# The down projection of pairs 1 to 8 in seven block products, spread between the products of gate and up, in a float32 encoder on one Trainium2 core

## The chip, the core and the metric

The kernel runs on one core of a Trainium2 chip. Its engines are named as the profile names them: PE (TensorE, matrix products; PEld is its loading of the stationary operand), DVE (VectorE), ACT (ScalarE), POOL (GpSimd) and SP (SyncE, which here only issues DMAs). The metric is the device time of one execution in microseconds (us); lower is better.

## The reference

Two layers of a hybrid encoder act on 768 tokens (512 of a sample, 256 of a prompt) of width 1024. Each layer has two feed-forward blocks with a mixer (attention and a state-space scan) between them. Only the feed-forward block is touched here:

```python
def swiglu_ffn(x, w_gate, w_up, w_down):
    return (jax.nn.silu(x @ w_gate) * (x @ w_up)) @ w_down

for l in range(DEPTH):                      # DEPTH = 2, D_FF = 2816
    x = layer_norm(ALPHA * x + 0.5 * swiglu_ffn(x, ...ffn1...), ln1_g[l], ln1_b[l])
    mix = hybrid_mixer(x, ...)
    x = layer_norm(ALPHA * x + mix, ln2_g[l], ln2_b[l])
    x = layer_norm(ALPHA * x + 0.5 * swiglu_ffn(x, ...ffn2...), ln3_g[l], ln3_b[l])
```

## The kernel before

**Arithmetic.** A float32 operand is held as two parts in the PE's format: a high part (an ACT cast) and a low part (DVE: the value less its high part). One product is three matmuls: high by high, high by low, low by high.

**Tiling.** The hidden width of 2816 is 22 tiles of 128, taken as 11 pairs p = 0 to 10; there are four such feed-forward stages. For a pair, gate and up are each a 2 by 2 block matrix times the input (tokens in two halves of 384, depth in two halves of 512). Pair 0 is plain (`plain_pair`). Pairs 1 to 10 (`fast_pair`) use the Strassen-Winograd form: seven block products instead of eight, 14 for gate and up together, each 4 x 3 = 12 matmuls of 384 columns (L444). The block sums of the input (T1 to T4) are made once per stage by `sums_of_x`, on DVE, ACT and POOL. Those of the weights, S1 to S4, are DVE additions of 128x512 (L89).

**Hidden values.** `block` evicts gate (silu on ACT) and up (a DVE product) into `sg`, a [128, 2, 768] buffer in the arena. `finish` (L366) splits all of `sg` into one of two `hbuf` pairs by one cast of 1536 columns on ACT (L368) and one subtraction on DVE (L369).

**Down.** `down` (L484) is one block of matmuls for a pair: for 6 token tiles, 2 hidden tiles and 3 part products into two banks of 512 columns, that is 72 matmuls of 512 columns (L499), each tile ending in two DVE evictions into `y` (L506). By `down_after` the block of pair 0 stands behind pair 0, the blocks of pairs 1 to 8 one pair late (that of pair p behind the products of pair p + 1), and those of pairs 9 and 10 together at the end.

**Weights.** `WeightStream` keeps the order of use. SP loads 1 MB slabs (two gate and up slabs and one down slab a pair) into two raw buffers. `split` makes the two parts of a unit of 128x512 (ACT L110, DVE L111) in one of nine rotating buffers, up to five units ahead. POOL issues no DMA.

**Order.** The program is written in order of dependence; a scheduler then sets the order of each engine's queue, in which instructions run strictly one after the other. Semaphores join the queues.

Of the kernel before, what the change touches and what calls it, by code (L numbers as in the profile page):

```python
# [50 lines left out]
class WeightStream:  # L51
    """Weights in the order of their use: DMA into raw slabs, then an exact split in two float32r parts.

    A unit is a slice of its slab, or a sum of slices (the block sums of a Strassen-Winograd product).
    """
# [36 lines left out]

    def split(self, upto):
        nc = self.nc
        while self.nsplit <= min(upto, len(self.units) - 1):
            u = self.units[self.nsplit]
            n = u.get("n", UNIT)
            self.dma(u["slab"] + 1)
            raw = self.source(u["slab"], u["what"], n)
            if u.get("place") is not None:  # L100
                hi, lo = self.places[u["place"]]
            else:
                t = self.pool.tile([P, 2 * ZN], F32R, tag="w", name="w", bufs=NWBUF)
                hi, lo = t[:, :n], t[:, n : 2 * n]
            g = u.get("scale")
            if g is not None:
                nc.scalar.activation(hi, raw, AF.Copy, scale=g)
                nc.vector.scalar_tensor_tensor(lo, raw, g, hi.bitcast(F32), op0=ALU.mult, op1=ALU.subtract)
            else:
                nc.scalar.copy(hi, raw)  # L110
                nc.vector.tensor_sub(lo, raw, hi.bitcast(F32))  # L111
            u["hl"] = (hi, lo)
            self.nsplit += 1

# [8 lines left out]
def trunk(ctx, tc, x_in, w_gu, w_dn, w_xbc, w_z, w_qk, w_v, w_out, ln_gb, ln_gbc, conv_wb, gmix, smalls, bias, y_out):  # L123
# [57 lines left out]
    # the order of the block products of gate (0) and up (1)  # L181
    PRODUCTS = ((0, 0), (0, 1), (0, "S2"), (0, "S1"), (0, "S3"), (1, 0), (0, 3), (0, "S4"),
                (1, "S2"), (1, 1), (1, "S3"), (1, "S1"), (1, 3), (1, "S4"))
    DCH = [(p, p + 1) for p in range(NPAIR - 2)] + [(NPAIR - 2, NPAIR)]

    def down_after(p):
        return [0] if p == 0 else [p - 1] if 1 < p < NPAIR - 1 else [len(DCH) - 1] if p == NPAIR - 1 else []

    for l in range(DEPTH):
        for w in range(2):  # L190
            if w == 1:
                slab(w_xbc[l, 0], range(4))
                for j in range(2):
                    slab(w_z[l, j], range(4), n=ZN)
                for j in range(1, 4):
                    slab(w_xbc[l, j], range(4))
                for j in range(4):
                    slab(w_qk[l, j], range(4))
                for j in range(2):
                    slab(w_v[l, j], range(4))  # L200
                for j in range(4):
                    i = slab(w_out[l, j])
                    for u in range(4):
                        k = 2 * j + u // 2
                        n = 4 * j + u - NWBUF
                        units.append(dict(slab=i, what=u, scale=gmx[:, l, k : k + 1], place=n if n >= 0 else None))
            dn = lambda a, b: [slab(w_dn[l, w, p], range(4)) for p in range(a, b)]
            for p in range(NPAIR):
                if p < NPLAIN:
                    a, b = slab(w_gu[l, w, p, 0]), slab(w_gu[l, w, p, 1])  # L210
                    units.extend(dict(slab=q, what=2 * m + k) for m in range(2) for q in (a, b) for k in range(2))
                else:
                    ab = slab(w_gu[l, w, p, 0]), slab(w_gu[l, w, p, 1])
                    units.extend(dict(slab=ab[m], what=x) for m, x in PRODUCTS)
                for c in down_after(p):
                    for i in range(*DCH[c]):
                        slab(w_dn[l, w, i], range(4))
    ws = WeightStream(nc, wpool, slabs, units, [at(o_sum + i * UNIT, UNIT) for i in range(3)])
# [5 lines left out]
    # ---- input  # L224
# [24 lines left out]
    def split_x(ps, k0, nk, c0, n):  # L249
        """PSUM columns -> the two parts of X"""  # L250
# [11 lines left out]
    def to_x(src, t, tags=("A", "A")):  # L262
        """token-major [128, 1024] -> X[:, :, tile t]"""
# [860 lines left out]
```

## Time and profile before

| | us |
|---|---|
| median of 3 runs | 2917.91 |
| lowest and highest run | 2914.05, 2918.11 |
| span of the profiled execution | 2913.6 |
| PE busy | 2869.5 (98%) |
| DVE busy | 1993.7 (68%) |
| ACT busy | 1300.1 (45%) |
| POOL busy | 135.5 (5%) |

Of the profiled execution the page gives the span alone; the runs lie 0.5 to 4.5 us above it, 4.3 at the median. Busy time counts from the start of an instruction to its end, and successive instructions of an engine overlap a little, so what an engine can take is read from the starts of instructions that follow one another without a wait. Start and end of matmuls are modelled; the distance of two starts is what one costs.

### The profile page before, as it was taken

Reading aid. Unit: us, or ns where it says so; the run is one execution under the profiler, and the core shown is the slowest. Engines: PE = TensorE matmul, PEld = TensorE weight load, DVE = VectorE, ACT = ScalarE, POOL = GpSimd, SP = SyncE. Lnnn points to the kernel's source line nnn. Section 1 sums busy time; section 2 is a strip of 40 time slices with the busy share of each in tenths; the row PEclk is TensorE's granted clock in tenths of the full one; section 3 lists DMA queues with packets and bytes.
Section 4 is the critical chain, followed back from the end, with each engine's and each line's share of the span. In section 5 each row is a group of like instructions: output and inputs, shape, how many; then the busy total and the mean of one; then the engine's idle time right before and its main releaser. Section 6 shows DMA issues by size and latency. Waiting matters only on the chain.

```text
span 2913.6 us, 39357 instructions
## 1 busy us (share of the span) xinstructions
PE 2869.5 (98%) x15382; PEld 2568.4 (88%) x15382; DVE 1993.7 (68%) x3659; ACT 1300.1 (45%) x2587; POOL 135.5 (5%) x193
## 2 busy tenths in 40 slices
PE   8999999999999999999989999999999999999998
PEld 7999999888767899999879999998887678999997
DVE  7767666868545966666697666667685459666666
ACT  4443333657456443333544333335583554433333
POOL 3000000100000100000030000000000011000000
PEclk9999999999999999999999999999999999999999
DMA  3221212224323121212212212222243231212212
GB/s 118 73 81 65 73 63 97 99 90 140 130 85 122 61 75 64 79 60 72 73 49 74 81 59 72 73 88 102 94 138 134 82 134 59 73 58 73 73 58 87
DMA packets 59451, 246.19 MB, mean 84 GB/s; under 512 B 7104, under 2 KB 19584, under 8 KB 37760
## 3 DMA queue, kind: packets, MB, share of 16 engines
q1 hardware_dynamic: 59264, 243.67, 24.4%
q8 instruction: 120, 1.97, 0.3%
q14 instruction: 67, 0.55, 0.1%
HBM read 224.67 MB, written 18.97 MB: 84 GB/s over the span
## 4 chain that ended last, share of the span: by engine, by line
PE 91%; DVE 5%; ACT 2%; issue 1%; POOL 1%; DMA 0%; SPq 0%; DVEq 0%; POOLq 0%; ACTq 0%
PE psA L444 40%; PE psB L499 12%; PE psC L499 12%; PE psA L346 6%; PE psA L848 5%; PE psA L1003 5%; PE psA L655 2%; PE psB L938 2%; PE psA L876 2%; PE psC L967 2%; PE psB L956 1%; DVE w L111 1%; PE psC L791 1%; PE psA L259 1%; PE psC L743 0%
## 5 line engine op out<-in xcount | busy, mean ns | idle before, releaser
L444 PE MATMUL psA<-XH,w 128*128 128x384 f32 x2560 | 701.4, 338 | 0.0
L110 ACT CAST w<-wraw 128x512 fp32r<-128x512 f32 (+1 forms) x544 | 333.1, 622 | 563.4 <-PE psB L499 381.3
L111 DVE TENSOR_TENSOR w<-wraw,w 128x512 fp32r<-128x512 f32 (+1 forms) x544 | 377.2, 703 | 252.2 <-ACT w L110 246.1
L444 PEld LDWEIGHTS psA<-XH,w 128*128 128x128 f32 x2560 | 468.2, 188 | 1.8
L444 PE MATMUL psA<-XL,w 128*128 128x384 f32 x1280 | 432.2, 338 | 0.0
L110 ACT CAST w<-arena 128x512 fp32r<-128x512 f32 x320 | 194.7, 621 | 216.1 <-PE psA L444 177.0
L111 DVE TENSOR_TENSOR w<-arena,w 128x512 fp32r<-128x512 f32 x320 | 216.9, 689 | 79.8 <-ACT w L110 67.4
L346 PE MATMUL psA<-XH,w 128*128 128x256 f32 (+1 forms) x1056 | 244.5, 338 | 4.9 <-DVE XH L311 4.9
L499 PE MATMUL psB<-w,h0h 128*128 128x512 f32 x576 | 229.7, 399 | 14.6 <-ACT h0h L368 14.6
L506 DVE SCALAR_TENSOR_TENSOR arena<-psB,arena 128x512 f32<-128x512 f32 x216 | 148.7, 688 | 139.0 <-PE psB L499 138.3
L444 PEld LDWEIGHTS psA<-XL,w 128*128 128x128 f32 x1280 | 240.7, 188 | 1.7
L499 PE MATMUL psC<-w,h0h 128*128 128x512 f32 x576 | 228.1, 396 | 0.0
L454 ACT COPY arena<-psA 128x384 f32<-128x384 f32 x240 | 115.1, 479 | 241.0 <-PE psA L444 241.0
L346 PEld LDWEIGHTS psA<-XH,w 128*128 128x128 f32 x1056 | 170.9, 192 | 27.3 <-DVE XH L311 6.3
L459 DVE TENSOR_TENSOR arena<-arena,psA 128x384 f32<-128x384 f32 x240 | 132.5, 552 | 84.1 <-ACT arena L454 45.8
L499 PE MATMUL psB<-w,h1h 128*128 128x512 f32 x480 | 189.5, 395 | 0.0
L499 PE MATMUL psC<-w,h1h 128*128 128x512 f32 x480 | 188.1, 392 | 0.0
L444 PE MATMUL psA<-T2h,w 128*128 128x384 f32 x640 | 177.2, 338 | 0.0
L444 PE MATMUL psA<-T4h,w 128*128 128x384 f32 x640 | 176.7, 337 | 0.0
L444 PE MATMUL psA<-T3h,w 128*128 128x384 f32 x640 | 176.4, 336 | 0.0
L346 PE MATMUL psA<-XL,w 128*128 128x256 f32 (+1 forms) x528 | 152.5, 338 | 3.3 <-DVE XL L312 3.3
L506 DVE SCALAR_TENSOR_TENSOR arena<-psC,arena 128x512 f32<-128x512 f32 x216 | 147.2, 681 | 0.0
(308 smaller groups left out, 5425.3 us busy)
## 6 DMA issues: line engine op xcount, KB each, us to landing
wraw<-in_w_gu_dram SPq DMA_DIRECT2D x86, 1024.0 KB, 4.9
wraw<-in_w_dn_dram SPq DMA_DIRECT2D x44, 1024.0 KB, 4.9
e<-ac_d SPq DMA_DIRECT2D x48, 256.0 KB, 3.4
wraw<-in_w_xbc_dram SPq DMA_DIRECT2D x8, 1024.0 KB, 4.9
wraw<-in_w_qk_dram SPq DMA_DIRECT2D x8, 1024.0 KB, 4.9
arena<-in_bias_dram SPq DMA_DIRECT2D x64, 128.0 KB, 2.1
wraw<-in_w_out_dram SPq DMA_DIRECT2D x8, 1024.0 KB, 4.8
arena<-in_ln_gb_dram SPq DMA_DIRECT2D x6, 1024.0 KB, 5.8
```

The lines of the kernel that those rows point to most:

```text
L110: nc.scalar.copy(hi, raw)
L111: nc.vector.tensor_sub(lo, raw, hi.bitcast(F32))
L346: t_.matmul(ps[:, o : o + b - a], w[:, k % 4], xx[:, k, a:b], start=(k == 0 and part == 0 and i == 0), stop=(k == KD - 1 and part == 1))
L444: t_.matmul(ps, wx[:, k], xx[:, k], start=first and k == 0 and i == 0, stop=k == 3 and i == 2, skip_group_check=not first)
L454: s_.copy(t, banks[m, 1])
L459: v_.tensor_add(src, src, ps)
L499: t_.matmul(ps[n], hx, units[2 * i + n][wx], start=(i == 0 and wi == 0), stop=(i == nf - 1 and wi == 2))
L506: v_.scalar_tensor_tensor(sl, ps[n], 0.5, sl, op0=ALU.mult, op1=ALU.add)
L655: t_.matmul(ps[:, : ZN // 2], xx[:, k % 4], wx[:, n * (ZN // 2) : (n + 1) * (ZN // 2)], start=(k == 0 and wi == 0), stop=(k == KD - 1 and ...
L848: t_.matmul(ps[r][:, : b - a], w[:, k % 4], xx[:, k, a:b], start=(k == 0 and part == 0 and i == 0), stop=(k == KD - 1 and part == 1))
L876: t_.matmul(ps, xx[:, k, cols], wx, start=(k == 0 and wi == 0), stop=(k == KD - 1 and wi == 2))
L1003: t_.matmul(p[n], xx[:, k, cols], wo[2 * k + n][wx], start=(i == 0 and wi == 0), stop=(i == KD - 1 and wi == 2))
```

## The change

Three things change together.

**Down in seven products.** For pairs 1 to 8 the hidden block matrix (tokens in two halves, hidden tiles in two) and the down weights (hidden tiles in two, columns in two) also go through the Strassen-Winograd form. `finish` now makes seven hidden parts of 128x384 (`hs`; A11, A12, A22 and four sums that POOL forms in place in `sg`), each with a cast and a subtraction. `split_down` makes seven weight parts with four DVE sums in place in the raw slab. `down_units` yields 21 pieces (three token tiles of 128 by seven products), each three matmuls of 512 columns and one DVE eviction into `y`. They are popped two at a time behind products 2 to 12 of the next pair. Pairs 0, 9 and 10 keep the plain form, with hidden parts of 384 columns.

**Low parts by transfers.** For units with `acc` (S1, S3 and S4 of gate and of up, and the last four of the seven down parts: ten a pair) the DVE subtraction goes. ACT writes minus the high part into the low part, and a DMA issued by POOL adds the raw value to it.

**Buffers.** Nine rotating weight buffers become twelve fixed places: five for gate and up, used in turn with four units ahead, and seven for down. Gate products are all ahead of up products now (before, they were interleaved).

```diff
+    def parts(self, raw, place, n=UNIT, acc=False, scale=None):
...
+        elif acc:
+            nc.scalar.copy(hi, raw)
+            nc.scalar.activation(lo, hi.bitcast(F32), AF.Copy, scale=-1.0)
+            nc.gpsimd.dma_start(lo, raw, accum_op=ALU.add)
...
+    def split_down(self, slab, i):
+        b11, b12, b21, b22 = (self.raw[slab][:, k * UNIT : (k + 1) * UNIT] for k in range(4))
+        sub = self.nc.vector.tensor_sub
+        if i == 2:
+            sub(b11, b12, b11)
+            sub(b12, b22, b12)
+        if i == 3:
+            sub(b11, b22, b11)
+        if i == 6:
+            sub(b21, b21, b11)
+        raw = (b11, b21, b11, b11, b22, b12, b21)[i]
+        return self.parts(raw, NGU + i, acc=i > 2)
...
+    PRODUCTS = [(m, x) for m in range(2) for x in (0, 1, "S2", "S1", "S3", 3, "S4")]
+    DOWN = (("A11", 1, ((0, 0),)), ("A12", 2, ((0, 0),)), ("S1", 3, ((1, 1),)), ("S2", 1, ((0, 1),)),
+            ("S4", 3, ((0, 1),)), ("S3", 1, ((1, 1),)), ("A22", 1, ((1, 0),)))
...
         def finish(p):
-            hh, hl = hbuf[p % 2]
-            s_.copy(hh, sg)
-            v_.tensor_sub(hl, sg, hh.bitcast(F32))
+            if p == 0 or p >= NPAIR - 2:
...
+            a11, a12, a21, a22 = hblock(0, ha), hblock(1, ha), hblock(0, hb), hblock(1, hb)
+            put_h(0, a11)
+            put_h(1, a12)
+            put_h(2, a22)
+            g_.tensor_add(a22, a21, a22)
+            g_.tensor_sub(a21, a11, a21)
+            put_h(3, a22)
+            g_.tensor_sub(a11, a22, a11)
+            put_h(4, a11)
+            g_.tensor_sub(a12, a12, a11)
+            put_h(5, a21)
+            put_h(6, a12)
...
-                product(ws.get(1, 5)[0], x, banks[m, b], first)
+                product(ws.get(1, NGU - 1)[0], x, banks[m, b], first)
...
+                if first_slab is not None:
+                    if i == 9:
+                        ws.dma(first_slab + 1)
+                    if i >= 10:
+                        dnw.setdefault(p, [])
+                        for k in range(2 * (i - 10), min(2 * (i - 9), NDN)):
+                            dnw[p].append(ws.split_down(first_slab, k))
+                if i >= 2:
+                    for _ in range(min(2, len(units_))):
+                        units_.pop(0)()
...
+        def down_units(p):
...
+                        for k, (hx, wx) in enumerate(((hh, wh), (hh, wl), (hl, wh))):
+                            t_.matmul(ps, hx, wx, start=first and k == 0, stop=k == 2, skip_group_check=not first)
+                        for half, n in blocks:
+                            sl = y[:, q + 3 * half, n * 512 : (n + 1) * 512]
+                            v_.scalar_tensor_tensor(sl, ps, 0.5, sl, op0=ALU.mult, op1=ALU.add)
```

Two places in the queues show the move. In all rows `w` is a weight part, `hNh` and `hNl` the high and low part of hidden part N (in the order of `put_h` after the change), `T3` a block sum of the input, `arena` holds `sg`, the weight sums and `y`.

The first place is the seam between two pairs. ACT before, where pair 3 of the first stage ends and pair 4 begins:

```order
L454 COPY arena<-psA 128x384
L110 CAST w<-wraw 128x512
L110 CAST w<-arena 128x512 x3
L368 CAST h1h<-arena 128x1536
L110 CAST w<-wraw 128x512 x2
```

ACT after, at the same seam (the order is the same at the later seams):

```order
L102 CAST w_100<-wraw 128x512
L103 ACTIVATE w_100<-w_100 128x512
L106 CAST w_90<-wraw 128x512
L512 COPY arena<-psA 128x384
L407 CAST h3h<-arena 128x384
L102 CAST w_89<-arena 128x512
L407 CAST h4h<-arena 128x384
L407 CAST h5h<-arena 128x384
L407 CAST h6h<-arena 128x384
L103 ACTIVATE w_89<-w_89 128x512
```

One cast of `sg` has become seven, of which the last four read what POOL forms; the negated copy for the unit in `w_89` (S3 of gate) now stands behind the last of them. POOL after, at the same seam (before, POOL had nothing between the pairs):

```order
L104 DMA w_93<-arena 128x512
L104 DMA w_100<-wraw 128x512
L420 TENSOR_TENSOR arena<-arena 128x384
L421 TENSOR_TENSOR arena<-arena 128x384
L423 TENSOR_TENSOR arena<-arena 128x384
L425 TENSOR_TENSOR arena<-arena 128x384
L104 DMA w_89<-arena 128x512
L104 DMA w_91<-arena 128x512
```

The transfer that completes `w_89` stands behind the four hidden sums; so it does at seven of the eight seams of a stage. PE after, in pair 4, up to the first use of `w_89`:

```order
L502 MATMUL psA<-XL,w_93 128x384
L502 MATMUL psA<-XH,w_93 128x384
L571 MATMUL psC<-w_96,h3h 128x512 x2
L571 MATMUL psC<-w_96,h3l 128x512
L571 MATMUL psB<-w_97,h4h 128x512 x2
L571 MATMUL psB<-w_97,h4l 128x512
L502 MATMUL psA<-T3h,w_89 128x384
L502 MATMUL psA<-T3l,w_89 128x384
```

The down pieces now stand between product 3 (`w_93`) and product 4 (`w_89`, with T3) of the next pair, not behind all fourteen.

The second place is the start of a stage, where pair 0 ends. PE before, from the last plain matmuls on (19 of L444 stand there in all, then the down block with h0):

```order
L346 MATMUL psA_406<-XH_67,w_393 128x512
L346 MATMUL psA_407<-XH_67,w_393 128x256
L444 MATMUL psA_696<-XH_67,w_634 128x384
L444 MATMUL psA_696<-XL_68,w_634 128x384
L444 MATMUL psA_696<-XH_67,w_634 128x384 x2
```

PE after, at the same place:

```order
L383 MATMUL psA_418<-XH_67,w3_92 128x512
L383 MATMUL psA_419<-XH_67,w3_92 128x256
L593 MATMUL psB_602<-w5_94,h0h_177 128x512
L593 MATMUL psC_603<-w6_95,h0h_177 128x512
L593 MATMUL psB_602<-w5_94,h0l_178 128x512
L593 MATMUL psC_603<-w6_95,h0l_178 128x512
L593 MATMUL psB_618<-w5_94,h0h_177 128x512
L593 MATMUL psC_619<-w6_95,h0h_177 128x512
L593 MATMUL psB_602<-w7_96,h1h_179 128x512
```

The first product of pair 1 is gone from ahead of the down block; eight matmuls with the first hidden tile stand there, and then the second hidden tile is needed.

## Rows read from the trace of the kernel before

**Rows 1.** The page, part 1: busy us (share of the span) xinstructions.

```profile
PE 2869.5 (98%) x15382; PEld 2568.4 (88%) x15382; DVE 1993.7 (68%) x3659; ACT 1300.1 (45%) x2587; POOL 135.5 (5%) x193
```

**Rows 2.** Busy time by stretch: stretch, its us, PE, PEld, DVE, ACT, POOL, clock, DMA.

```profile
276.00:322.00 46.00, 46.00 (x242) 42.95 (x241) 31.29 (x50) 16.67 (x29) 0.00 (x0) 1.00 0.20 69
```

**Rows 3.** Timeline, ACT, the cast of the hidden values (start, us, instruction, [idle before]).

```profile
318.41 1.48 ACT L368 CAST h0h<-arena 128x1536 fp32r<-128x1536 f32 x1 [1.63 <-DVE arena L463]
...
364.43 1.48 ACT L368 CAST h1h<-arena 128x1536 fp32r<-128x1536 f32 x1 [1.63 <-DVE arena L463]
```

**Rows 4.** Timeline, PE, starts of two products and of two token tiles of down.

```profile
290.73 0.34 PE L444 MATMUL psA<-T2h,w 128*128 128x384 f32 x1
...
292.84 0.34 PE L444 MATMUL psA<-XH,w 128*128 128x384 f32 x1
...
315.96 0.39 PE L499 MATMUL psB<-w,h1h 128*128 128x512 f32 x1
...
318.73 0.40 PE L499 MATMUL psB<-w,h1h 128*128 128x512 f32 x1
```

**Rows 5.** Timeline, DVE, instructions that follow one another, 384 and 512 columns.

```profile
290.93 0.55 DVE L459 TENSOR_TENSOR arena<-arena,psA 128x384 f32<-128x384 f32 x1 [0.27 <-PE psA L444]
...
317.83 0.55 DVE L463 TENSOR_TENSOR arena<-arena 128x384 f32<-128x384 f32 x1
318.30 0.68 DVE L89 TENSOR_TENSOR arena<-arena,wraw 128x512 f32<-128x512 f32 x1
318.90 0.68 DVE L506 SCALAR_TENSOR_TENSOR arena<-psB,arena 128x512 f32<-128x512 f32 x1
```

**Rows 6.** Timeline, ACT, 384 and 512 columns (the x2 row: two casts).

```profile
305.71 0.48 ACT L454 COPY arena<-psA 128x384 f32<-128x384 f32 x1 [0.93 <-PE psA L444]
306.08 0.62 ACT L110 CAST w<-wraw 128x512 fp32r<-128x512 f32 x1
...
331.12 1.15 ACT L110 CAST w<-wraw 128x512 fp32r<-128x512 f32 x2 [11.23 <-PE psB L499]
```

**Rows 7.** Timeline, POOL, sums of 384 columns in `sums_of_x`, first stage.

```profile
35.70 7.43 POOL L427 TENSOR_TENSOR arena<-XL 128x384 f32<-128x384 f32 x1 [4.84 <-DVE T3l L416]
43.09 1.02 POOL L424 TENSOR_TENSOR arena<-XH,XL 128x384 f32<-128x384 f32 x1
...
46.66 1.33 POOL L424 TENSOR_TENSOR arena<-XH,XL 128x384 f32<-128x384 f32 x1
```

**Rows 8.** Timeline, DVE, beside those of rows 7.

```profile
40.37 1.88 DVE L111 TENSOR_TENSOR w<-wraw,w 128x512 fp32r<-128x512 f32 x3
43.30 1.22 DVE L416 TENSOR_TENSOR XL<-arena,XH 128x384 fp32r<-128x384 f32 x1 [1.05 <-ACT XH L415]
...
47.03 1.37 DVE L428 TENSOR_TENSOR arena<-arena 128x384 f32<-128x384 f32 x1
```

**Rows 9.** DMA issues: line, count, KB each, median us from issue to landing.

```profile
e<-ac_d SPq DMA_DIRECT2D x48, 256.0 KB, 3.4
...
sz_d<-arena SPq DMA_DIRECT2D x12, 256.0 KB, 2.0
arena<-sz_d SPq DMA_DIRECT2D x12, 256.0 KB, 2.7
```

**Rows 10.** Timeline, PE, the first matmul of down behind pair 0, four stages.

```profile
57.00 0.80 PE L499 MATMUL psB<-w,h0h 128*128 128x512 f32 x1 [3.62 <-ACT h0h L368]
57.59 0.63 PE L499 MATMUL psC<-w,h0h 128*128 128x512 f32 x1
...
980.40 0.50 PE L499 MATMUL psB<-w,h0h 128*128 128x512 f32 x1 [1.57 <-ACT h0h L368]
...
1507.54 0.80 PE L499 MATMUL psB<-w,h0h 128*128 128x512 f32 x1 [7.81 <-ACT h0h L368]
...
2431.55 0.50 PE L499 MATMUL psB<-w,h0h 128*128 128x512 f32 x1 [1.63 <-ACT h0h L368]
```

**Rows 11.** Busy time by stretch behind the first two of rows 10 (columns as rows 2).

```profile
57.00:60.00 3.00, 3.00 (x7) 2.44 (x8) 3.00 (x5) 1.15 (x3) 0.00 (x0) 0.50 0.00 0
60.00:63.00 3.00, 3.00 (x9) 2.41 (x9) 0.99 (x2) 1.65 (x3) 0.00 (x0) 0.52 0.00 0
980.00:990.00 10.00, 9.60 (x42) 7.86 (x43) 9.65 (x16) 3.96 (x9) 0.00 (x0) 1.00 0.00 0
```

More of the change, by code (lines that the diff above doesn't have):

```diff
@@ L97, in split @@
             n = u.get("n", UNIT)
-            self.dma(u["slab"] + 1)
+            self.dma(u["slab"] + u.get("next", 1))
             raw = self.source(u["slab"], u["what"], n)
[L100 to L112, printed above, removed]
-            self.nsplit += 1
+            u["hl"] = self.parts(raw, u["place"], n, u.get("acc", False), u.get("scale"))
+            self.nsplit += 1
+    def split_down(self, slab, i):
[10 more added lines that the diff above has]
+        return self.parts(raw, NGU + i, acc=i > 2)
     def get(self, n=1, ahead=0):
@@ L203, in trunk @@
                     for u in range(4):
[L204 to L207, printed above, removed]
+                        k, n = 2 * j + u // 2, 4 * j + u
+                        units.append(dict(slab=i, what=u, scale=gmx[:, l, k : k + 1], place=n - 8 if n >= 8 else n + 8))
@@ L208, in trunk @@
+                ring[0] = NGU - 1
             for p in range(NPAIR):
-                if p < NPLAIN:
-                    a, b = slab(w_gu[l, w, p, 0]), slab(w_gu[l, w, p, 1])
-                    units.extend(dict(slab=q, what=2 * m + k) for m in range(2) for q in (a, b) for k in range(2))
-                else:
[L213 to L217, printed above, removed]
@@ L218, in trunk @@
-    ws = WeightStream(nc, wpool, slabs, units, [at(o_sum + i * UNIT, UNIT) for i in range(3)])
+                a, b = slab(w_gu[l, w, p, 0]), slab(w_gu[l, w, p, 1])
+                if p == 0:
+                    units.extend(dict(slab=q, what=2 * m + k, place=cyc(NGU)) for m in range(2) for q in (a, b) for k in range(2))
+                    slab(w_dn[l, w, p], range(4))
+                    for k, u in enumerate(units[-4:]):
+                        u["place"] = NGU + k
+                else:
+                    ab = (a, b)
+                    units.extend(dict(slab=ab[m], what=x, acc=x in ("S1", "S3", "S4"), place=cyc(NGU), next=int(i >= NGU - 1))
+                                 for i, (m, x) in enumerate(PRODUCTS))
+                    if p < NPAIR - 2:
+                        dn_slab[l, w, p] = slab(w_dn[l, w, p])
@@ L220, in trunk @@
+            for p in range(NPAIR - 2, NPAIR):
+                slab(w_dn[l, w, p], range(4))
+            for k, u in enumerate(units[-8:]):
+                u["place"] = NGU + k if k < NDN else NGU - 1
+            ring[0] = NGU - 1 if w == 1 else NW - 1
+    wt = [pers.tile([P, 2 * ZN], F32R, name=f"w{i}") for i in range(NW)]
+    ws = WeightStream(nc, wpool, slabs, units, [at(o_sum + i * UNIT, UNIT) for i in range(3)], wt)
     y = at(o_y, NT * DM).rearrange("p (t d) -> p t d", t=NT)
@@ L354, in ffn @@
         hpool = hp.enter_context(tc.tile_pool(name="hpool", bufs=1))
-        hbuf = [tuple(hpool.tile([P, 2, T], F32R, name=f"h{i}{j}") for j in "hl") for i in range(2)]
+        hs = [tuple(hpool.tile([P, HT], F32R, name=f"h{i}{j}") for j in "hl") for i in range(8)]
         tpool = tp.enter_context(tc.tile_pool(name="tpool", bufs=1))
@@ L481, in fast_pair, with run, down @@
                     saved[m, "d"] = True
-            finish(p)
-        def down(c):
-            a, b = DCH[c]
-            last = c == len(DCH) - 1
+                if first_slab is not None:
[8 more added lines that the diff above has]
+                        units_.pop(0)()
+            assert not units_
+            finish(p)
+        dnw = {}
+        def down_units(p):
+            out = []
+            for q in range(3):
+                banks = {}
+                for i, (part, b, blocks) in enumerate(DOWN):
+                    def run(q=q, i=i, part=part, b=b, blocks=blocks, banks=banks):
+                        first = b not in banks
+                        if first:
+                            banks[b] = bank("B" if b == 1 else "C")
+                        ps = banks[b]
+                        hh, hl = (x[:, q * P : (q + 1) * P] for x in hs[HPART[part]])
+                        wh, wl = dnw[p][i]
+                        for k, (hx, wx) in enumerate(((hh, wh), (hh, wl), (hl, wh))):
[3 more added lines that the diff above has]
+                            v_.scalar_tensor_tensor(sl, ps, 0.5, sl, op0=ALU.mult, op1=ALU.add)
+                    out.append(run)
+            return out
+        def down(a, b):
+            last = b == NPAIR
             nf = 2 * (b - a)
```

92 lines of the change are left out of this document (56 added, 36 removed).

## The prediction

> **What bounds the kernel now.** I read the page's busy times first: PE is busy 98% of the span [rows 1]. That is a mean, so I then read one pair in the middle of a stage by the busy time of its stretch: 46.00 of 46.00 us on PE, DVE 31.29, ACT 16.67, POOL nothing, the clock at 1.00, which is the upper of its two levels (2.4 GHz) [rows 2]. In these stretches only fewer matmuls, or shorter ones, save time. The period of a pair is the distance of two casts of the hidden values, 364.43 - 318.41 = 46.02 us [rows 3]. It is made up of 14 products of 292.84 - 290.73 = 2.11 us each (12 matmuls, 0.176 each), 29.5 us, and six token tiles of down of 318.73 - 315.96 = 2.77 us each (12 matmuls, 0.23 each), 16.6 us [rows 4]; the two make 46.1.
>
> **What the change takes away.** Down of a pair goes from 72 matmuls to 3 x 7 x 3 = 63. Nine matmuls of 0.23 us are 2.07 us a pair; 8 pairs in 4 stages are 32, so 66.2 us go from PE. All of it lies on the bounding engine. PE's floor for a pair becomes 29.5 + 63 x 0.23 = 44.0 us.
>
> **What it adds to DVE and ACT.** Instructions of 512 columns follow each other on DVE in 0.60 us, of 384 in 0.47 [rows 5]. Before, a pair has 18 low parts, 8 sums and 12 evictions of 512, ten of 384 and one of 1536: 38 x 0.60 + 10 x 0.47 + 1.7 = 29 us. After, it has 11 low parts, 12 sums and 21 evictions of 512, ten and seven of 384: 44 x 0.60 + 17 x 0.47 = 34.4 us of 44. ACT: 21 casts and 10 negated copies of 512 at 0.53 (a pair of casts takes 1.15, less the overlap) and 17 of 384 at 0.37 to 0.43 [rows 6], about 23 us of 44. Neither becomes the bound by its sum; I cost these at nothing, with PE's 44 us as the cover. Where that cover is thin is the order, at the seam.
>
> **The seam, step by step** (time from the end of a pair's last product, t = 0). Product 4 of the next pair needs the S3 unit, whose place is freed only by that last product. PE gets there after four products and four down pieces: 4 x 2.11 + 12 x 0.23 = 11.2, and the low part is wanted two matmuls later, at t = 11.55. Ahead of that low part stand, each queue in its order:
> - DVE: 0.2 after the product (an addition started 290.93 - 290.73 = 0.2 behind the start of PE's next product [rows 4, 5]), then add, h1l, multiply, h2l. Three distances of 0.47 and one full 0.55 make 2.2. Only then may POOL overwrite the block.
> - POOL: four hidden sums. Such an addition takes 1.02 alone and 1.33 in turn with DVE [rows 7], whose own 0.55 becomes 1.22 to 1.37 at the same time [rows 8]. I take 4 x 1.33, because DVE has low parts to make there, and 0.6 for one DVE instruction ahead of the first: 5.9, so t = 8.1. The bounds are 4 x 1.02 (t = 6.3) and a longer hold, below.
> - ACT: the cast of h6 (0.37) and behind it the negated copy (0.62), 1.0: t = 9.1.
> - The adding transfer, 256 KB, from POOL's queue. No row shows one. The nearest are SP's transfers of 256 KB: 2.0, 2.7 and 3.4 us to landing [rows 9]. Bounds: 2.0, and 3.4 with another 1.0 for POOL (one of its own additions in rows 7), 4.4. A gain is excluded, as PE waits for the landing or doesn't. I take 3.2, near the upper row, because POOL must issue it and it reads its target too: t = 12.3.
>
> The low part is then 0.8 us late. The order has this at seven seams of a stage, 28 in all (at the first, the transfer stands ahead of the four sums): 28 x 0.8 = 22 us come back. The other nine transfers of a pair either stand ahead of the hidden sums or are wanted two products later and more; copy, negated copy and transfer are 0.6 + 0.6 + 3.2 = 4.4 us against four products, at least 8.4, so they cost nothing while POOL issues them in time. Behind the waiting transfer POOL has only that of S4, and ACT has S4's cast and the copy of product 2's bank, which PE needs for product 4 anyway.
>
> A page of the Trainium skill (DMA: Bandwidth & Descriptors, section Anatomy of one DMA — SWDGE (gpsimd) path) prices a transfer from POOL's queue at about 2.0 us plus its bytes over 436 GB/s. Worked out from it (an estimate) this one takes 2.6 us, the low part is 0.15 us late, and the sum below would be 18 us lower. No run here shows such a transfer yet, and an addition may cost more than a copy.
>
> **The start of a stage.** Before, the first product of pair 1 (20 matmuls of 0.176, 3.5 us) covers part of the wait for the hidden cast; still PE idles 3.62, 1.57, 7.81 and 1.63 us [rows 10]. After, 8 matmuls of 0.23 (1.8 us) stand there, then PE needs the second hidden tile. It hangs on the same multiply, with a cast of 384 columns for one of 1536 (1.0 sooner) but with two hidden and two weight low parts more ahead of it on DVE (2.1 later). Loss: 3.5 - 1.8 + 1.1 = 2.8 us, in four stages 11 us. Bounds: 0 if DVE waits there anyway, 23 if the short idle times grow to where the clock falls (below). I take 11, the sum from the order.
>
> **The sum.** Against the profiled span: 2913.6 - 66.2 + 22 + 11 = 2880.4; the median of the runs lies 4.3 above that span, so 2884.7, 33 us or 1.1% below the median.
>
> **Rivals.**
> 1. The transfers are hidden: POOL's sums at 1.02 and a transfer of 2.0 to 2.7 land at t = 9.3 to 10.0. Then 2917.9 - 66.2 + 0 to 11 = 2852 to 2863. For it: POOL shows 1.02. Against it: rows 7 and 8 show POOL and DVE in each other's way wherever both work.
> 2. The wait gives all back: at (66.2 - 11) / 28 = 1.97 us a seam the time is that of before. It needs t = 13.5, so 1.2 more than I take, well inside the bounds. Between 1.75 and 2.2 it is 2912 to 2924.
> 3. Slower, by a longer wait at the same seam: with the transfer at 4.4 and two DVE instructions more in POOL's way (1.2), t is 14.7, 3.1 late: 2917.9 - 66.2 + 88 + 11 = 2951. From 2.2 us late on this decides.
> 4. Much slower, by the clock: behind an idle time of 3.62 us PE ran at 0.50 and 0.52 of its clock (the lower level, 1.2 GHz) for some 6 us, but at 1.00 behind 1.57 [rows 10, 11]. That loses about 2.9 us more. If POOL's sums are held as one was, 7.43 us, while DVE ran low parts without a pause [rows 7, 8], the wait reaches 3.6 and more: 28 x (3.6 + 2.9) = 182, so 2917.9 - 66.2 + 182 + 23 = 3057. Against it: DVE itself waits for these sums at the seam, so it must pause. Of POOL's issuing, a page of the Trainium skill (SBUF — State Buffer, section SBUF: two separate sides) says that DVE instructions in its two-port mode keep POOL from writing a transfer's descriptors, and names a copy within SBUF as such; the pair has none of these on DVE, so by the page the issue itself isn't held, and this rival rests on the sums alone.
> 5. The change doesn't do what it says, or the pieces don't fit between the products: the order shows 63 down matmuls a pair in place, so only 1 in 100.
>
> **How the numbers follow.** A difference of 0.2% (about 6 us) is what a measurement of this kernel can tell from no change. My forecast, a partial gain between 2864 and 2912, has 0.37, and 2885 is its value. Rival 1 has 0.18, rival 2 0.12, rival 3 0.20, rival 4 0.12, rival 5 (no change) 0.01. Faster by over 0.2%: 0.37 + 0.18 = 0.55. Within: 0.12 + 0.01 = 0.13. Slower: 0.20 + 0.12 = 0.32. The range goes from 2856, the middle of rival 1, to 2965, the far side of rival 3; about 0.08 lie below and 0.12, rival 4, above.
>
> **What would show it.** In a pair of the changed kernel: the period by the first hidden cast, 44.0 + 0.8; the waits of PE at T3 with the low part, released by a POOL transfer, and its time from issue to landing; POOL's four sums at the seam, 1.0 or 1.3 each or far longer; DVE near 34 us a pair by starts; PE's clock at 1.00. I am wrong if PE waits elsewhere, on a bank of the down pieces or on DVE, if the transfer lands in under 2.4 us or takes over 4.4, or if the clock falls in the pairs.

## The result and the profile after

| | before | after |
|---|---|---|
| median, us | 2916.8 (4 runs) | 3128.8 (4 runs) |
| span of the profiled execution | 2913.6 | 3131.5 |
| PE busy | 2869.5 | 2905.8 |
| PE idle (span less busy) | 44.1 | 225.7 |
| mean granted clock | 0.995 | 0.962 |

After is slower by 7.3%: the ratio is 1.0731, with a 95% interval of 1.0716 to 1.0747. The forecast was 2885.

The page of after, part 1 (busy us, share, instructions; before: [rows 1]), its DMA issues (count, KB each, median us to landing), and its waits of PE (us in total, times, longest):

```profile
PE 2905.8 (93%) x15094; PEld 2567.7 (82%) x15094; DVE 2223.1 (71%) x4031; ACT 1588.3 (51%) x3279; POOL 597.5 (19%) x689
...
w<-arena POOLq DMA_DIRECT2D x240, 256.0 KB, 4.0
...
w<-wraw POOLq DMA_DIRECT2D x128, 256.0 KB, 4.3
...
PE psA L502 <- DMA w<-arena: 129.1, 30, 5.8
PE psB L593 <- ACT h1h L407: 24.7, 4, 6.6
PE psA L502 <- ACT w L106: 13.9, 4, 3.7
```

Nine matmuls a pair are gone (15382 - 15094 = 288 = 9 x 32), yet PE was busy 36 us longer. One pair, from one cast of h1 to the next, and its seam (columns as [rows 2]):

```profile
206.75:258.67 51.92, 47.15 (x233) 42.81 (x232) 39.37 (x62) 24.79 (x50) 13.83 (x15) 0.93 0.47 112
...
219.00:223.50 4.50, 0.23 (x2) 0.00 (x0) 0.42 (x1) 0.87 (x2) 0.02 (x1) 0.76 1.02 237
223.50:230.00 6.50, 6.44 (x22) 5.80 (x23) 5.05 (x9) 1.52 (x3) 0.00 (x0) 0.64 0.03 6
```

A pair takes 51.9 us, before 46.0 [rows 2, 3]. PE stands still for over 4 us and then runs at 0.64 of its clock, the lower level for most of the stretch. The timeline of that seam, all engines (start, us, instruction, [idle before <- what ended it]):

```profile
209.89 1.34 POOL L420 TENSOR_TENSOR arena<-arena 128x384 f32<-128x384 f32 x1
...
213.73 0.33 SPq L69 DMA_DIRECT2D wraw<-in_w_gu_dram  x1
...
214.03 1.35 POOL L425 TENSOR_TENSOR arena<-arena 128x384 f32<-128x384 f32 x1
...
214.56 0.33 SPq L69 DMA_DIRECT2D wraw<-in_w_dn_dram  x1
...
215.41 0.51 ACT L407 CAST h6h<-arena 128x384 fp32r<-128x384 f32 x1 [0.50 <-POOL arena L425]
...
215.82 0.63 ACT L103 ACTIVATE w<-w 128x512 fp32r<-128x512 f32 x1
...
216.90 0.88 POOL L104 DMA_DIRECT2D w<-arena  x1 [1.52 <-PE psA L502]
...
223.56 1.01 PE L502 MATMUL psA<-T3h,w 128*128 128x384 f32 x2 [4.33 <-DMA w<-arena]
...
224.95 0.69 DVE L90 TENSOR_TENSOR arena<-wraw 128x512 f32<-128x512 f32 x1 [5.53 <-DMA w<-arena]
```

The transfer of gate's S3 part is issued at 216.90 and lands 6.6 us later (the view of L104 gives 6.6 for this one). PE waits 4.33 us for it, DVE 5.53 us, because a sum of up's weights may not overwrite one that a transfer still reads. The wait of PE is there at 28 seams, 3.8 to 5.8 us each; that is 127 of the 129.1 us. The down slab, issued 2.3 us ahead of the transfer, lands at 222.3, the transfer 1.2 us behind it.

**Where 218 us of span went.** Idle time grew by 181.6: some 127 at the seams, 10 at the stage starts (24.7 less the 14.6 of [rows 10]), 14 in the second fast pair of each stage (ACT w L106), the rest in waits of 2.5 us and less. Busy time grew by 36.3, although the work shrank by 67 (the last run below has PE busy 2802.4): so some 103 us were lost at the lower clock. Spread over 28 seams, 4 starts and 4 second pairs, that is 2.9 us each on the mean.

### The profile page after: what moved, and what is told of

It reads as the page before. It is cut to its first block, busy times and chain, and to the rows that moved or that the text cites. A ratio compares the mean times of both kernels' runs of the same rounds, so it can differ in the third digit from the quotient of the medians.

```text
span 3131.5 us, 41384 instructions
## 1 busy us (share of the span) xinstructions
PE 2905.8 (93%) x15094; PEld 2567.7 (82%) x15094; DVE 2223.1 (71%) x4031; ACT 1588.3 (51%) x3279; POOL 597.5 (19%) x689
## 3 DMA queue, kind: packets, MB, share of 16 engines
q1 hardware_dynamic: 59264, 243.67, 23.1%
q0 software_dynamic: 52992, 96.49, 17.7%
## 4 chain that ended last, share of the span: by engine, by line
PE 59%; DVE 14%; DMA 12%; issue 7%; POOL 5%; ACT 3%; POOLq 0%; DVEq 0%; SPq 0%; ACTq 0%
PE psA L502 19%; DMA w<-arena 9%; PE psA L383 5%; PE psB L571 5%; PE psA L1094 5%; PE psC L571 4%; PE psA L940 4%; DVE w L107 3%; PE psB L593 2%; PE psC L593 2%; DVE arena L574 2%; PE psA L747 2%; PE psB L1029 2%; PE psA L967 2%; PE psC L1058 2%
## 5 line engine op out<-in xcount | busy, mean ns | idle before, releaser
L106 ACT CAST w<-wraw 128x512 fp32r<-128x512 f32 (+1 forms) x512 | 308.8, 620 | 332.7 <-PE psA L502 203.5
L104 POOL DMA_DIRECT2D w<-arena x240 | 213.2, 888 | 1110.8 <-ACT w L103 461.2
L502 PE MATMUL psA<-T3h,w 128*128 128x384 f32 x640 | 214.9, 402 | 130.9 <-DMA w<-arena 127.2
L574 DVE SCALAR_TENSOR_TENSOR arena<-psB,arena 128x512 f32<-128x512 f32 x384 | 262.6, 684 | 41.6 <-PE psB L571 40.6
L90 DVE TENSOR_TENSOR arena<-wraw 128x512 f32<-128x512 f32 x160 | 110.2, 689 | 239.6 <-DMA w<-arena 190.6
L102 ACT CAST w<-arena 128x512 fp32r<-128x512 f32 x240 | 148.2, 618 | 239.6 <-PE psA L502 221.5
L502 PEld LDWEIGHTS psA<-T3h,w 128*128 128x128 f32 x640 | 141.1, 230 | 144.8 <-DMA w<-arena 136.5
L103 ACT ACTIVATE w<-w 128x512 fp32r<-128x512 f32 x368 | 225.2, 628 | 3.9
L512 ACT COPY arena<-psA 128x384 f32<-128x384 f32 x240 | 113.2, 472 | 210.0 <-PE psA L502 210.0
L574 DVE SCALAR_TENSOR_TENSOR arena<-psC,arena 128x512 f32<-128x512 f32 x288 | 194.6, 685 | 13.0 <-PE psC L571 6.6
L306 POOL TENSOR_TENSOR stat<-stat,cst 128x1 f32<-128x1 f32 x60 | 26.2, 437 | 885.1 <-ACT arena L908 415.5
L104 POOL DMA_DIRECT2D w<-wraw x128 | 110.6, 921 | 398.7 <-DVE wraw L127 274.1
```

The lines of the kernel that those rows point to most:

```text
L103: nc.scalar.activation(lo, hi.bitcast(F32), AF.Copy, scale=-1.0)
L104: nc.gpsimd.dma_start(lo, raw, accum_op=ALU.add)
L502: t_.matmul(ps, wx[:, k], xx[:, k], start=first and k == 0 and i == 0, stop=k == 3 and i == 2, skip_group_check=not first)
L574: v_.scalar_tensor_tensor(sl, ps, 0.5, sl, op0=ALU.mult, op1=ALU.add)
```

## The experiments

Every time stands beside about 2915 us of before on the same chip.

**One part undone: S3 by VectorE (e1).**

```diff
-acc=x in ("S1", "S3", "S4")
+acc=x in ("S1", "S4") or (x == "S3" and m == 1)
```

> One part undone: the low part of gate's S3 alone is made by a VectorE subtraction again (0.68 us), the other nine still by adding transfers. Theory (seam): 28 seams lose the 4.5 us that PE waits for the landing of this low part and the 2.9 us that each half-clock stretch behind it costs, 28 x 7.4 = 207, so 3129 - 207 = 2922 us, clock back at 0.985 or more. Rival (all transfers are late): the wait moves to gate's S4, whose transfer is issued 1.3 us after, and over half stays: 3020 us or more. Rival (VectorE bound): VectorE, held by the sum temps that transfers still read, is late at the evictions, 1 to 2 us a pair: 2950 to 2980 us.

Measured 3111.1 us. My theory fell. The wait at T3 is gone, and 3.1 us stand a few instructions later. PE's largest wait, and the timeline at the seam:

```profile
PE psC L571 <- DVE arena L574: 108.5, 33, 5.7
...
223.90 0.69 DVE L90 TENSOR_TENSOR arena<-wraw 128x512 f32<-128x512 f32 x1 [2.99 <-DMA w<-arena]
...
225.85 0.50 PE L571 MATMUL psC<-w,h6h 128*128 128x512 f32 x1 [3.13 <-DVE arena L574]
```

DVE's queue runs in order. A sum (L90) waits for a temporary that S4's transfer still reads, the evictions (L574) stand behind it, and PE waits for their bank. The late transfers have two victims, PE and DVE. My second rival had named DVE and these evictions, but at 1 to 2 us a pair; it is 3.1 us here and 108.5 in all, so the time came out far above that rival's.

**Why the transfer lands late (e2, e5, e14, e13).** Rows of after put two slab loads of 1 MB 2.3 and 3.2 us ahead of it. In e2 and e5 the down slab was to be held by a DVE write into its buffer, behind product 5 and 7; the scheduler put both writes at the same early place.

```diff
+if hold:
+    self.nc.vector.memset(t[:, :1], 0.0)
 self.nc.sync.dma_start(t[:, : ap.shape[1]], ap)
...
-next=int(i >= NGU - 1)
+next=int(i >= NGU - 1 and (i < 7 or p >= NPAIR - 2))
...
+if i == 5:
+    ws.dma(first_slab, hold=True)
```

e5 has `i == 7` where e2 has `i == 5`.

> All ten transfers stay; only the load of the next down slab (1 MB), which SyncE issues 2 to 3 us ahead of the late transfer, is held until after product 5 by a VectorE write of one column into the slab's buffer. Theory (DMA engines shared): the transfer's time to landing falls from 6.6 us to about 3.2 to 3.5, PE waits about 1.2 us, the clock doesn't fall: 3129 - 28 x (3.3 + 2.9) = 2955 us. Rival (the transfer is slow by itself, its issue and its own queue): landing stays at 6 us and more, 3120 to 3135 us.

> All as in the changed kernel, but the load of the next down slab is held until after product 7, some 9 us behind the late transfer instead of 2.3 us ahead of it (held until after product 5 it started 0.4 us behind, and the transfer took 7.7 us to land). Theory (the transfer shares the DMA engines with the slab and comes last): landing of gate's S3 part 3.5 to 4.2 us after its issue, PE waits 1 to 1.7 us, no fall of the clock: 3129 - 28 x (3 + 2.9) = 2965 us. Rival (the transfer is slow by itself, or VectorE's wait for the sum temps is the true limit): 3080 us or more.

Measured 3148.5 and 3143.8 us: the load starts 0.4 us behind the transfer, which in e2 then takes 7.7 us. The hold didn't do its work, so this decides nothing. e14 ties the load to the result of the waiting product:

```diff
-next=int(i >= NGU - 1)
+next=int(i >= NGU - 1 and (i < 7 or p >= NPAIR - 2))
...
+if i == 5:
+    ws.dma(first_slab, after=saved[0, "S3"][:, :8])
...
+if after is not None:
+    self.nc.sync.dma_start(t[:, :8], after)
```

> All ten transfers and the order of PE, ACT, VectorE and POOL almost as in the changed kernel; the load of the next down slab is made to follow the product that waits (a 4 KB transfer out of that product's saved result into the slab's buffer goes ahead of it). The two holds before did not move it: the load started 0.4 us behind the late transfer. Theory (the late transfer lands last because it shares the DMA engines with the slab loads issued 2.3 and 3.2 us ahead of it): landing 3.3 to 4 us after the issue instead of 6.6, PE waits 1 to 1.7 us, no fall of the clock, 3129 - 28 x (3 + 2.9) = 2965 us. Rival (transfer slow by itself): landing 6 us or more, 3120 us or more.

Measured 3067.4 us. Timeline of e14 at the seam (its lines stand 2 below those of after):

```profile
212.41 0.88 POOL L106 DMA_DIRECT2D w<-arena  x1 [1.52 <-PE psA L504]
...
215.78 0.62 PE L504 MATMUL psA<-T3h,w 128*128 128x384 f32 x2 [1.05 <-DMA w<-arena]
...
217.35 0.69 DVE L92 TENSOR_TENSOR arena<-wraw 128x512 f32<-128x512 f32 x1 [2.59 <-DMA w<-arena]
...
219.30 0.73 PE L575 MATMUL psC<-w,h6h 128*128 128x512 f32 x2 [1.50 <-DVE arena L578]
...
223.21 0.34 SPq L71 DMA_DIRECT2D wraw<-in_w_dn_dram  x1
```

The transfer lands in 3.3 us, PE waits 1.05, and the clock stays at 1.00 through the whole pair. That part of the theory holds at this seam. Over the whole kernel these waits are 0.9 to 5.5 us, 55.5 in all where after has 129.1; the longest stand at the last seam of a stage. The larger part of the 100 us that I missed is the other victim: DVE still waits for temporaries, PE 1.50 us for the eviction here and 1.89 us again later in the pair, where the moved load meets the next transfer (5.9 us to landing). PE waits 60.5 us for such evictions in all. e13 adds load instead:

```diff
 put_h(6, a12)
+for i in (2, 3, 4, 5):
+    nc.sync.dma_start(extra_d[i], hs[i][0].bitcast(F32))
```

> The other way round: at each seam four h blocks (768 KB) are also copied to a DRAM buffer that nobody reads, on SyncE's queue ahead of the two slab loads, which so start some 1 to 2 us later too. Theory (sharing): landing of the late transfer 8.5 to 10 us, PE waits 2 to 3.5 us more at 28 seams: 3185 to 3230 us. Rival: landing stays at 6.6 us, 3130 us.

Measured 3182.2 us. Timeline of e13 (the last line shows the wait):

```profile
221.63 0.33 SPq L69 DMA_DIRECT2D wraw<-in_w_gu_dram  x1
...
222.06 0.40 SPq L69 DMA_DIRECT2D wraw<-in_w_dn_dram  x1
...
222.99 0.88 POOL L104 DMA_DIRECT2D w<-arena  x1 [1.53 <-PE psA L505]
...
231.60 1.01 PE L505 MATMUL psA<-T3h,w 128*128 128x384 f32 x2 [6.27 <-DMA w<-arena]
```

The transfer takes 8.6 us, PE waits 6.27. The edit did two things: it added load, and it put the slabs 1.4 and 0.9 us ahead of the transfer instead of 3.2 and 2.3. Both go the same way. With little beside it the transfer takes 3.3 us, beside two slabs 6.6, with more load and later slabs 8.6: what else the DMA engines carry sets the landing time.

**Where the chain ahead of it can be cut (e3, e18).** e3 moves the four hidden sums from POOL to DVE:

```diff
-g_.tensor_add(a22, a21, a22)
-g_.tensor_sub(a21, a11, a21)
+v_.tensor_add(a22, a21, a22)
+v_.tensor_sub(a21, a11, a21)
...
-g_.tensor_sub(a11, a22, a11)
+v_.tensor_sub(a11, a22, a11)
...
-g_.tensor_sub(a12, a12, a11)
+v_.tensor_sub(a12, a12, a11)
```

> The four sums of the hidden blocks go from POOL to VectorE (0.55 us each for 1.3). Theory: the chain ahead of the late transfer shortens by 1.5 to 4 us, with the slab loads in front of it as they are the landing comes 2 to 2.6 us late, below the wait after which the clock falls: about 2995 us. If the transfer only queues behind the slabs and lands when they are done, whenever it is issued: 3120 us, no change. If VectorE is the bound, slower than 3129.

Measured 2936.3 us: 193 of the 212 us are back. Timeline of e3:

```profile
209.01 0.86 POOL L104 DMA_DIRECT2D w<-arena  x1 [1.98 <-DVE h3l L408]
...
210.91 0.33 SPq L69 DMA_DIRECT2D wraw<-in_w_gu_dram  x1
...
212.55 0.33 SPq L69 DMA_DIRECT2D wraw<-in_w_dn_dram  x1
...
215.10 0.34 PE L502 MATMUL psA<-T3h,w 128*128 128x384 f32 x1
```

The transfer now leaves 6.1 us ahead of PE's first matmul with T3 (1.8 in after), ahead of both slabs, and lands in 3.3 us; PE doesn't wait. I had expected about 2 us of wait: the gain in the issue also won the race with the slabs. e18 leaves the sums on POOL and shortens the transfers of the down parts instead:

```diff
-return self.parts(raw, NGU + i, acc=i > 2)
+return self.parts(raw, NGU + i, acc=i in (3, 4))
```

> One part of the change undone alone: the down parts of blocks 5 and 6 by VectorE, eight adding transfers left, the hidden sums on POOL as in the changed kernel. The slab's buffer is free some 4 us earlier, so both slab loads start ahead of POOL's sums and are over, or nearly, when gate's S3 transfer is issued. Theory (sharing with the slab loads made the transfer late): it lands in 3.3 to 4 us, PE waits 1 to 1.7 us without a fall of the clock: 2950 to 2985 us. Rival (POOL's sums alone make it late): no cure, 3100 us or more.

Measured 3154.0 us, no cure. Timeline of e18:

```profile
213.19 1.93 POOL L420 TENSOR_TENSOR arena<-arena 128x384 f32<-128x384 f32 x1 [2.81 <-DVE h2l L408]
...
219.96 0.87 POOL L104 DMA_DIRECT2D w<-arena  x1 [1.37 <-PE psC L571]
...
220.61 0.33 SPq L69 DMA_DIRECT2D wraw<-in_w_dn_dram  x1
...
226.65 1.01 PE L502 MATMUL psA<-T3h,w 128*128 128x384 f32 x2 [4.08 <-DMA w<-arena]
```

DVE has more ahead of h2l, so POOL's sums start later, and the transfer meets the down slab again (6.6 us). PE also gets a new wait of 1.2 us at each seam, put down to an ACT cast (L102), 33.2 in all. Both theories named half: POOL's sums make the issue late, and late means beside the slab.

**Fewer transfers, sums still on POOL (e4, e9).** e4 has the first of these two edits, e9 both.

```diff
-acc=x in ("S1", "S3", "S4")
+acc=False
...
-return self.parts(raw, NGU + i, acc=i > 2)
+return self.parts(raw, NGU + i, acc=False)
```

> All six low parts of gate and up by VectorE, adding transfers for the four down parts alone. VectorE gets 6 x 0.68 = 4.1 us more a pair, 43.5 of some 44.2. Theory: no seam wait, evictions sometimes late: about 2930 us. Rival (VectorE bound): a pair takes 46 us or more: 2970 us or more. It says what the six transfers of gate and up are worth when the seam is cured.

> One part of the change alone: seven down products, hidden sums on POOL, and no adding transfer at all (all ten low parts by VectorE). VectorE gets 10 x 0.68 = 6.8 us more a pair than in the changed kernel, some 46 us of work for a pair whose products take 43.9. Theory: VectorE bounds the pair, which takes 46 to 48 us: 2960 to 3010 us. Rival (the transfers were of no use): the down parts free their slab earlier, the pair takes 45 us: 2925 us or less.

Measured 2979.4 and 2998.6 us: with no transfer at all the loss is still 83 us. I took that for DVE's bound. PE's largest wait in e4, the timeline of e9 at a seam and the clock right behind it (columns as [rows 2]) say otherwise:

```profile
PE psB L571 <- ACT w L106: 58.5, 28, 2.1
...
302.65 1.93 POOL L420 TENSOR_TENSOR arena<-arena 128x384 f32<-128x384 f32 x1 [41.03 <-DVE h2l L408]
...
304.62 0.51 ACT L407 CAST h3h<-arena 128x384 fp32r<-128x384 f32 x1 [3.90 <-POOL arena L420]
...
306.02 1.50 DVE L107 TENSOR_TENSOR w<-arena,w 128x512 fp32r<-128x512 f32 x1
...
309.35 0.44 PE L502 MATMUL psA<-T3h,w 128*128 128x384 f32 x1 [1.64 <-ACT arena L512]
...
311.45 1.22 PE L571 MATMUL psB<-w,h4h 128*128 128x512 f32 x2 [0.96 <-DVE arena L574]
...
311.00:314.00 3.00, 2.54 (x7) 2.26 (x8) 3.00 (x6) 0.97 (x2) 0.00 (x0) 0.50 0.74 221
```

ACT and DVE wait in order for POOL's sums, with the copy of PE's bank (L512) and the weight parts behind them, and DVE's instructions stretch from 0.68 to 1.50 us beside POOL's. In e4 PE's wait behind ACT stands at all 28 seams. So the sums on POOL hold up PE without any late transfer too; making the ten low parts by transfers adds 130 us to that (2998.6 to 3128.8).

**With the sums on DVE, where the rest is (e7, e8, e11, e12).** All four have e3's edit. e7: the first fast pair's down parts by DVE.

```diff
-return self.parts(raw, NGU + i, acc=i > 2)
+return self.parts(raw, NGU + i, acc=acc and i > 2)
...
-dnw[p].append(ws.split_down(first_slab, k))
+dnw[p].append(ws.split_down(first_slab, k, p > 1))
```

e8 is e7 and the down products of the first pair ahead of the sums of X; in this order the sums overwrite weight sums that pair 1 has yet to read, so it computes something else and its time stands for the order alone.

```diff
-sums_of_x()
 down(0, 1)
+sums_of_x()
```

e11 has two low parts by transfer in place of four, e12 has that and the edit of e1.

```diff
-return self.parts(raw, NGU + i, acc=i > 2)
+return self.parts(raw, NGU + i, acc=i in (3, 4))
```

> The kernel with the hidden sums on VectorE (2936 us), and in the first fast pair of each stage alone the four transfers of the down parts replaced by VectorE subtractions, so that the slab's buffer is free earlier and the next up slab is loaded earlier. Theory: the wait of 3.3 to 3.8 us in the second fast pair of the four stages goes, with the half clock behind it (2.9 us) and the late eviction there (0.4 to 2 us): 2936 - 4 x 7 = 2908 us. Rival: VectorE is late there instead: 2930 to 2940 us.

> As the run before, and at the start of a stage the products of the first pair's down projection are emitted ahead of the sums of X, so that VectorE multiplies and splits h before those sums. Theory: the wait of 5.2 to 6.6 us at the four stage starts falls to 2 to 3 us, the half clock behind it shortens: 2908 - 4 x 5 = 2888 us, faster than before (2917). Rival: the sums of X come late for the second and third product, and the wait moves there: 2905 to 2920 us.

> The kernel with the hidden sums on VectorE (2936 us), and only the first two of the four transferred down parts by transfers (the last two, of blocks 5 and 6, by VectorE: 1.36 us a pair more). Theory: the down slab's buffer is free some 4 us earlier, the next up slab comes earlier, the late evictions (14 us) and the waits of the second pairs (14 us and the clock behind them) shrink: 2895 to 2915 us. Rival (VectorE bound): 2940 us or more.

> As the run before, and gate's S3 part by VectorE too (0.68 us a pair more): five transfers a pair... seven of ten are left, S1 and S4 of both, S3 of up, two down parts. Theory: no product at the seam waits for a transfer, in the second pair of a stage either: 2890 to 2910 us. Rival (VectorE bound, as 46 us without any transfer gave 2999): 2930 us or more.

Measured 2942.8, 2929.3, 2915.0 and 2920.6 us. e7 and e12 gave nothing: in e7 a wait for S3's transfer took the place of the one removed, and e12 is 6 us slower than e11. e8 is 13 us below e7; its four waits at the starts fall from 24.6 to 14.9 us. e11 has PE busy without a gap in the middle of a stage (45.00 of 45.00 us), a pair takes (421.34 - 156.49) / 6 = 44.1 us by the cast of h1, and yet the total only equals before. So the pairs gave their 1.9 us each, some 61 us in 32 pairs, and the two ends of the stages must have lost it again; the next three runs test that.

**The two ends of a stage (e15, e16, e17).** e15 is e11 with the three POOL sums of `sums_of_x` on DVE.

```diff
-g_.tensor_add(f22, h22, l22)
-g_.tensor_add(f21, h21, l21)
+v_.tensor_add(f22, h22, l22)
+v_.tensor_add(f21, h21, l21)
...
-g_.tensor_sub(t3, l12, l11)
+v_.tensor_sub(t3, l12, l11)
```

e16 is e11 with e7's second edit and no adding transfer for gate and up in the pairs at the two ends; e17 is e15 and e16 together.

```diff
-return self.parts(raw, NGU + i, acc=i > 2)
+return self.parts(raw, NGU + i, acc=acc and i in (3, 4))
...
-acc=x in ("S1", "S3", "S4")
+acc=1 < p < NPAIR - 2 and x in ("S1", "S3", "S4")
```

> The kernel with hidden sums on VectorE and two of the down parts by transfers (2915 us), with the sums of X at the start of a stage on VectorE too (0.55 us each for 1.3 on POOL). There VectorE's own sums take 1.26 to 1.37 us beside POOL's and 0.54 us alone, and the product of gate and up that the down projection waits for stands behind them. Theory: the wait of 5.2 to 6.7 us at the four stage starts falls by 1.5 to 3 us: 2903 to 2909 us. Rival: VectorE has the 12 sums more and is later still: 2920 us.

> The kernel of 2915 us with adding transfers in pairs 2 to 8 alone: the first fast pair and the last two of each stage, which have no evictions of hidden products, get all their low parts from VectorE. Theory: the waits there (3 us behind DVE sums that waited for a buffer, 1 us for the slab, 3.5 us in the last two pairs for ScalarE, which makes the negated copies) go: 4 x 5 = 20 us, 2895 us. Rival (VectorE is the bound there): 2920 us or more.

> Both of the last two edits. Theory: 2885 us (2875 to 2895), 1% faster than before. Rival: one of them costs as much as the other gains: 2905 to 2915 us.

Measured 2892.5, 2871.6 and 2847.4 us, each better than expected, so the ends did hold it: 67 us come back. At a start of after, DVE works beside POOL's sums, then through its own, and only then multiplies:

```profile
45.26 1.37 DVE L474 TENSOR_TENSOR T4l<-arena,T4h 128x384 fp32r<-128x384 f32 x1
...
46.70 1.40 POOL L483 TENSOR_TENSOR arena<-XH,XL 128x384 f32<-128x384 f32 x1 [0.49 <-DVE T4l L474]
...
55.99 1.01 DVE L442 TENSOR_TENSOR arena<-arena,psA 128x512 f32<-128x512 f32 x2
...
57.43 0.80 PE L593 MATMUL psB<-w,h1h 128*128 128x512 f32 x1 [6.21 <-ACT h1h L407]
```

In e17 that multiply starts at 49.30, and of the four waits (24.7 us) 2.8 us are left; waits of 7.0 us in all for evictions of the same block (L593 <- DVE arena L602) are new.

**What of this is the change's (e19, e20).** e19 is the kernel before with the edit of e15. e20 is e17 with `acc=False` everywhere: the seven products alone, no adding transfer, no sum on POOL (the edits of e3, e9 and e15).

> The kernel before with one edit that has nothing to do with the change: the sums of X at the start of a stage on VectorE instead of POOL. It tells how much of the 2847 us is the seven products' and how much this edit's. Theory (the edit gains what the waits at the four starts cost, 14.6 us before, and the half clock behind them): 2917 - 10 = 2905 us (2895 to 2912). Rival: it was worth 22 to 24 us in the changed kernel and is worth the same here: 2893 us, so that the seven products give 46 us of the 69.

> The kernel of 2847 us without any adding transfer: all low parts by VectorE, which has 5 in a pair more (3.4 us), the hidden sums there too. VectorE would be busy some 43 us of a pair of 44. Theory (VectorE near its bound, evictions late): 2870 to 2900 us. Rival (the transfers were of no use, their waits cost what they spare): 2845 us or less.

Measured 2903.3 us (ratio 0.9961, 0.9946 to 0.9976) and 2842.1 us (0.9752, 0.9735 to 0.9768). The page of e20, part 1, and a pair of it:

```profile
PE 2802.4 (99%) x15094; PEld 2504.8 (88%) x15094; DVE 2357.2 (83%) x4575; ACT 1416.7 (50%) x2911; POOL 62.2 (2%) x145
...
231.45:275.68 44.23, 44.23 (x233) 41.24 (x232) 42.78 (x77) 20.29 (x40) 0.00 (x0) 1.00 0.21 72
```

So e20 beats before by 2.5% and after by 287 us. It is not slower than e17 with eight transfers a pair in pairs 2 to 8 (2847.4, and eight, not the five that I counted above; ratio 0.9768, 0.9752 to 0.9784; the intervals overlap): there the transfers spare DVE nothing that PE would feel. From e19 to e20 the seven products are worth 2903.3 - 2842.1 = 61 us, together with the new buffers and the new order of gate and up, which no run separates. Of the 157 us between e9 and e20, both without transfers, the sums of X account for 22 (e11 to e15) to 24 (e16 to e17), so the hidden sums on POOL cost about 133 us. That is a difference of differences: no run without transfers moves the hidden sums alone.

## Why the prediction was wrong

**PE's saving: right.** 66.2 us were forecast; PE's busy time falls by 2869.5 - 2802.4 = 67.1 in e20, and from e19 to e20 the time falls by 61.

**The seam: the place was right, one term was not.** The last product ends at 207.0 (two products of 2.11 ahead of 211.26). From there POOL's sums begin at 2.9 us (forecast 2.8), end at 8.3 (8.1), and the negated copy is done at 9.4 (9.1); the issue comes at 9.9. The sums were neither held nor at 1.02: the first takes 1.34. Then the step that failed: "the adding transfer, 256 KB ... I take 3.2", bounds 2.0 to 4.4. It took 6.6. So PE waits 3.8 to 5.8 us at a seam, not 0.8, and the seams cost 127 us of waiting, not 22. The value of 3.2 is right with little else in flight (3.3 in e3 and e14). My rows [rows 9] give medians of other transfers at other places (those of 3.4 range from 3.1 to 5.3), and I did not look at which loads SP issues at t = 6.7 and 7.5. The price of the Trainium skill (DMA: Bandwidth & Descriptors, section Anatomy of one DMA — SWDGE (gpsimd) path), 2.6 us by estimate, is also below both. The Trainium skill (the same page, section Queues, rings and completion order) says that each DMA engine takes turns between its queues packet by packet. The traces agree that the two queues share: the small transfer takes twice as long beside the slabs. Why the small one lands even behind the down slab (223.5 after 222.3), no run shows.

**The clock: the mechanism of rival 4, by another cause.** A long wait, then time lost at the lower level: the waits measured 3.8 to 5.8 us, the loss behind each 2.9. But I tied that rival to a long hold of POOL's sums and gave it 0.12; the transfer alone sufficed. With 4.5 us and 2.9 us at 28 seams in place of its 3.6 and 2.9, its own sum gives 2917.9 - 66.2 + 207 + 23 = 3082, 47 below the time that came. The second fast pairs (14 us and the clock behind them) and waits of 2.5 us and less, which it does not have, make up most of that.

**The other nine transfers, put at nothing: wrong.** I asked when PE wants their result, not who waits for what they read. In after DVE waits 257 us in all for sum temporaries (L90). e1 shows what this is worth when PE's wait at T3 is gone: 3111 us, only 18 less.

**"I cost these at nothing, with PE's 44 us as the cover": right by the sum, wrong at the seam.** DVE runs at 42.78 of 44.23 us in e20 without a loss. But POOL's four sums were priced only for the chain to S3's low part. ACT and DVE wait for them in order, with PE's bank copies and weight parts behind, and e9 loses 83 us to before without one transfer. So this step would have failed even with a transfer of 3.2 us. For the 34.4 us of DVE with the transfers the pair of after shows 39.37, stretched by POOL and by overlap in the count of busy time.

**The start of a stage: the sum is right by luck.** 11 us more were forecast, 2.8 at each start, and 10.1 measured. But the four waits went from 3.62, 1.57, 7.81 and 1.63 [rows 10] to 6.21, 6.55, 5.30 and 6.63: three grew by 2.6 to 5.0, one fell by 2.5. The lower clock stands behind all four now, behind two before, which the 11 does not hold; the case of "23 if the short idle times grow to where the clock falls" was the nearer one.

## What to carry over

Price a transfer at the place where it will run: look at what every other queue has in flight when it is issued, and take the time beside those loads, not the quiet one. An asynchronous step has two sets of waiters: who needs what it writes, and who may not yet overwrite what it reads; behind an in-order queue the second can cost as much. Before work is moved to a spare engine, ask whether its result stands in a chain that an in-order queue waits for: here small sums cost least on the busiest helper, DVE, and low parts cost no more there than by transfers, with DVE busy 97% of the pair.

## What the hardware showed unexpectedly

- An adding transfer of 256 KB within SBUF lands 3.3 us after its issue with little else in flight, 6.6 beside two loads of 1 MB, 8.6 with 768 KB more and the loads issued later. Its packets took 17.7% of 16 engines' span for 368 transfers, 24 engine-us each; the SP queue's, at 23.1% for 243.7 MB, took 12.5 for as many bytes. So a byte of these transfers occupies the engines about twice as long. Whether the adding does that is not shown: their packets are also half as large (1.8 KB on the mean for 4.1), and no run has such a transfer without the adding.
- A DVE subtraction of 384 columns takes 0.55 us alone and 1.37 beside a POOL sum, one of 512 columns 0.68 and 1.50. The Trainium skill (SBUF — State Buffer, section SBUF: two separate sides) says that a DVE instruction with two SBUF inputs and a POOL instruction that reads SBUF lock each other out of a shared port; the traces agree, as these instructions stretch side by side. The Trainium skill (GPSIMD Engine Reference, section Engine selection) would have elementwise sums on VectorE; e3 and e15 agree, by 193 and 22 us.
- Behind a wait of 4.33 us PE ran at the lower clock; behind 1.05 and 1.50 us in e14 (ending at 215.78 and 219.30) it stayed at 1.00. In e9 it ran at 0.50 behind 1.64 and 0.96 us (ending at 309.35 and 311.45), so the length of one wait does not settle it.
